# Another order for the attention of layer 0: after a run of half-width matmuls TensorE takes other full-width work ahead of new stick-breaking logits

## The chip, the cores and the metric

The kernel runs on one core of one Trainium2 chip. The metric is the device time of one execution in microseconds; the time before is the median of three runs. TensorE is written PE, VectorE DVE, ScalarE ACT, GpSimd POOL, and the engine whose queue issues most transfers SP.

## What is computed

A decoder trunk of two layers on 2,074 positions (16 learned meta tokens, 2,048 real ones, and padding). Only layer 0's attention is touched by the change. It has two groups of eight heads that read the same input, a stick-breaking attention and an MLA softmax attention:

```
def stick_breaking_attention(q, k, v):
...
        z = jnp.einsum('bthd,bshd->bhts', q[:, q0:q1], k[:, :q1]).astype(jnp.float32) * scale
...
        log_beta = jax.nn.log_sigmoid(z)
        log_1m = jnp.where(mask, log_beta - z, 0.0)
        suffix = lax.cumsum(log_1m, axis=3, reverse=True) - log_1m
        a = jnp.where(mask, jnp.exp(log_beta + suffix), 0.0)
        outs.append(jnp.einsum('bhts,bshd->bthd', a.astype(v.dtype), v[:, :q1]))
...
def causal_block_softmax_attention(q, k, v, scale):
...
        p = jax.nn.softmax(jnp.where(mask, s, NEG), axis=-1)
        outs.append(jnp.einsum('bhts,bshd->bthd', p.astype(v.dtype), v[:, :q1]))
```

The suffix sum makes a stick-breaking block depend on the block after it along the keys, so the key blocks of one query group are worked one after the other. The softmax has no such chain.

## The kernel before, in words

The program has three large parts one after the other: the projections of layer 0, its attention (here the stage from 722 to 1560 us of the profiled execution), and its output projection with all of layer 1. The change acts on the attention alone.

The 17 blocks of 122 positions are cut into query groups, one of one block (group 0) and four of four blocks (groups 1 to 4, 488 columns wide). The eight heads of each kind are worked as four pairs. For a pair and a group the kernel goes through steps, one key block of each kind a step; group 4 has 17 steps, group 3 has 13, then 9, 5 and 1. The groups of a pair run from 4 down to 0 (in the last pair 4, 0, 3, 2, 1). The first four steps of a long group are on the diagonal, so their stick-breaking part has 122, 244, 366 and 488 columns; all later ones have 488.

One step gives these operations, each for head m = 0 and 1 of the pair (the kinds are the names in the planner's tables):

- qks: stick-breaking logits, two matmuls into a PSUM tile zp (L1048, L1049); z masks the diagonal (L1056, DVE).
- e: softplus of zp into sp (L1060, ACT); c: one row of sp is overwritten with the running sum of the step before, read from that step's zp (L1067, ACT); h: sp rounded (L1075 on DVE, or L1073 on ACT); lo: the rest, sp minus h, into l (L1080, POOL or DVE).
- tri: two matmuls that add the triangular sums of h and l into the same zp (L1085, L1086); a: the weights from zp (L1090, ACT).
- qkm: MLA logits, three matmuls into ms (L1118 to L1120); p: their exponent (L1124, ACT); pm masks the diagonal (L1130, DVE); acc adds p up for the denominator (L1136, L1138, POOL).
- avs and avm: the products with the values, for both heads at once (L1098, L1146). Each head has 64 outputs, so each of these matmuls uses half of PE's columns: these, and dn (L1158, the denominators), are the half-width ones. The trace shows four records for one avs or avm, all other matmuls are full-width with one record.

So there is a chain per head: tri of a step, then c, h, lo and tri of the next step, with PE, ACT, DVE and POOL in turn.

The order is not written by hand. attention_plan makes the 4,320 operations with costs, dependences and the buffers that each takes and frees (two zp tiles for each head, for example), and list_schedule plays them through: whenever an engine is free it takes the ready operation with the smallest key. The key is the step's number plus RANK of the kind. A half-width operation gets RANK's few added when fewer than two of its sort are ready, and RANK's stay taken off while PE is in a run of them, which keeps half-width work together; TURN is what the planner charges for entering a run. MOVE says how long the owning engine must still be busy before lo or acc goes to its other engine. The order that comes out is binding on PE, ACT, DVE and POOL. SP's queue is not planned here; it follows the order in which the loads are written, which is where their operations stand in the plan: a group's q tile (a DMA from d_sq) is loaded when the last qks of the group before the last has been placed, since there are two q buffers; mq likewise behind qkm. The keys and values of the next pair are loaded when groups 4, 3 and 2 of the current pair are done (RELOAD), so there are such loads during the first three pairs and none during the last.

Of the kernel before, what the change touches and what calls it, by code (L numbers as in the profile page):

```python
# [126 lines left out]
def attention_plan():  # L127
# [115 lines left out]
    for o in ops:  # L243
        for d, w in o.deps:
# [4 lines left out]
DMA_NS = 6000  # L249
RINGS = dict(zp0=2, zp1=2, a0=3, a1=3, sp0=2, sp1=2, h0=2, h1=2, l0=2, l1=2, av=1, mav=1, ms=2,  # L250
             p0=3, p1=3, acc0=3, acc1=3, og=2, rd=1)
RANK = dict(qks=-48.53, z=-16.4, e=36.5, rc=-42.98, c=-9.66, h=11.42, lo=-30.91, tri=-5.03, a=4.01, avs=5.07, avm=3.11, ogs=23.02, qkm=-2.2, p=-10.76, pm=2.07, acc=-41.78, ogm=12.82, dn=-0.45, rd=8.86, rm=-7.51, head=0.23, other=11.93, few=12.47, stay=8.39)
MOVE = dict(lo=829, acc=3122, h=0)
HEAD = {("lo", "tri"): -200, ("a", "avs"): -40, ("p", "avm"): -40}
HALF_WIDTH = ("avs", "avm", "dn")
TURN = 342
# [5 lines left out]

def list_schedule(ops, rank=RANK, move=MOVE, rings=RINGS):

    engines = ("PE", "ACT", "DVE", "Pool")
    held = {r: [] for r in rings}
    users, wait, rt, pri = {}, {}, {}, {}
    ready = {e: [] for e in engines}
    for i, o in enumerate(ops):
        wait[o], rt[o] = len(o.deps), 0  # L270
        pri[o] = (o.s.i + rank[o.kind] + rank["head"] * o.m, i)
        for b in o.rel:
            users[b] = b.users
        if not o.deps:
            ready[o.eng].append(o)
    busy = {e: 0 for e in engines}
    out, events, tick, now, half = [], [], 0, 0, False
    while len(out) < len(ops):
        again = True
        while again:  # L280
            again = False
            for e in engines:
                if busy[e] > now:
                    continue
                best = None
                if e == "PE":
                    few = rank["few"] * (sum(o.kind in HALF_WIDTH and rt[o] <= now for o in ready[e]) < 2)
                for src in engines:
                    for o in ready[src]:
                        own = src == e  # L290
                        if rt[o] > now or not own and (not o.alt or o.alt[0] != e or busy[src] - now < move[o.kind]):
                            continue
                        if any(len(held[b.ring]) >= rings[b.ring] and users[held[b.ring][-rings[b.ring]]] for b in o.acq):
                            continue
                        k = (pri[o][0] + (0 if own else rank["other"]), pri[o][1])
                        if o.kind in HALF_WIDTH:
                            k = (k[0] - rank["stay"] if half else k[0] + few, k[1])
                        if best is None or k < best[0]:
                            best = (k, o, src)
                if best:  # L300
                    _, o, src = best
                    ready[src].remove(o)
                    for b in o.acq:
                        held[b.ring].append(b)
                    o.on, o.start = e, now
                    o.took = o.cost if src == e else o.alt[1]
                    if e == "PE":
                        o.took += TURN * (o.kind in HALF_WIDTH and not half)
                        half = o.kind in HALF_WIDTH
                    busy[e] = now + o.took  # L310
                    tick += 1
                    heapq.heappush(events, (busy[e], tick, "end", o))
                    out.append(o)
                    again = True
        if not events:
            break
        while True:
            now, _, what, x = heapq.heappop(events)
            if what == "end":
                for y, w in x.outs:  # L320
                    wait[y] -= 1
                    rt[y] = max(rt[y], now + w + LAT[x.on, y.eng])
                    if wait[y] == 0:
                        ready[y.eng].append(y)
                        tick += 1
                        heapq.heappush(events, (rt[y], tick, "ready", y))
                for b in x.rel:
                    tick += 1
                    heapq.heappush(events, (now + 200, tick, "free", b))
            elif what == "free":  # L330
                users[x] -= 1
            if not events or events[0][0] > now:
                break
    assert len(out) == len(ops)
    return out
# [5 lines left out]
def build(tc, a, off, upto=99):  # L341
# [113 lines left out]
    b2 = ExitStack()  # L455
    MSC = float((NOPE + ROPE) ** -0.5)
    plan = list_schedule(attention_plan())
    groups = sorted({o.s.G.i: o.s.G for o in plan}.values(), key=lambda g: g.i)
    slots = dict(big=0, small=0)
# [1462 lines left out]
```

## Time and profile before

| | |
|---|---|
| three runs | 2561.8, 2563.64 (median), 2575.18 us |
| profiled execution | 2566.46 us, its span 2564.7 us |
| attention in it | 722 to 1560 us |
| PE, DVE, ACT, POOL busy over the span | 98%, 59%, 51%, 41% |
| TensorE clock granted, mean | 0.995 |

Matmuls are pipelined: the next one starts while the last is still in the array, and a record's length is more than the distance to the next start. So "busy" says little about PE here, and the distances between starts say what a matmul costs. An idle time that is printed for PE is what is left after the modelled end of the matmul before; the distance of the starts is longer.

### The profile page before, as it was taken

Reading aid. Unit: us, or ns where it says so; the run is one execution under the profiler, and the core shown is the slowest. Engines: PE = TensorE matmul, PEld = TensorE weight load, DVE = VectorE, ACT = ScalarE, POOL = GpSimd, SP = SyncE. Lnnn points to the kernel's source line nnn. Section 1 sums busy time; section 2 is a strip of 40 time slices with the busy share of each in tenths; the row PEclk is TensorE's granted clock in tenths of the full one; section 3 lists DMA queues with packets and bytes.
Section 4 is the critical chain, followed back from the end, with each engine's and each line's share of the span. In section 5 each row is a group of like instructions: output and inputs, shape, how many; then the busy total and the mean of one; then the engine's idle time right before and its main releaser. Section 6 shows DMA issues by size and latency. Waiting matters only on the chain.

```text
span 2564.7 us, 38785 instructions
## 1 busy us (share of the span) xinstructions
PE 2525.8 (98%) x13105; PEld 1968.7 (77%) x13105; DVE 1523.6 (59%) x3356; ACT 1313.0 (51%) x3347; POOL 1042.5 (41%) x848
## 2 busy tenths in 40 slices
PE   9999999999999999999999999999999999999998
PEld 7887888999966666666666666788999888777776
DVE  5365486878435565565575665434222678888874
ACT  6532121213258878878878783423222577665442
POOL 1022200010058878878878776300000123356552
PEclk9999999999999999999999999999999999999999
DMA  5476744342576361252330214534554455676652
GB/s 149 108 200 174 198 115 109 93 119 81 132 166 146 82 157 44 78 144 51 91 102 22 66 61 143 168 91 139 128 124 120 123 134 137 162 206 190 202 164 92
DMA packets 337857, 321.29 MB, mean 125 GB/s; under 512 B 143670, under 2 KB 319738, under 8 KB 337075
## 3 DMA queue, kind: packets, MB, share of 16 engines
q1 hardware_dynamic: 336939, 317.56, 46.0%
q8 instruction: 103, 1.69, 0.3%
q10 hardware_dynamic: 720, 1.26, 0.1%
q14 instruction: 95, 0.78, 0.1%
HBM read 198.28 MB, written 120.80 MB: 124 GB/s over the span
## 4 chain that ended last, share of the span: by engine, by line
PE 90%; DVE 3%; DMA 3%; SPq 1%; issue 1%; ACT 1%; POOL 1%; ACTq 0%; DVEq 0%; POOLq 0%
PE psd L419 8%; PE psd L420 8%; PE psd L421 8%; PE pso L1797 7%; PE psg L1684 6%; PE av L1098 5%; PE mav L1146 5%; PE zp L1048 4%; PE psx L967 3%; PE zp L1086 3%; PE zp L1085 3%; PE zp L1049 3%; PE pso L1275 2%; PE ms L1118 2%; PE pso L1273 2%; PE ms L1119 2%
## 5 line engine op out<-in xcount | busy, mean ns | idle before, releaser
L1624 POOL TENSOR_TENSOR s_sb<-s_sb,den 108x1008 f32<-108x1008 f32 (+1 forms) x76 | 151.7, 1995 | 513.4 <-DVE den L1623 459.0
L1080 POOL TENSOR_TENSOR l<-sp,h 123x488 fp32r<-123x488 f32 (+3 forms) x253 | 292.9, 1164 | 106.1 <-DVE h L1075 86.9
L1075 DVE CAST h<-sp 123x488 fp32r<-123x488 f32 (+3 forms) x266 | 178.4, 676 | 252.7 <-ACT sp L1067 234.3
L1138 POOL TENSOR_TENSOR acc<-acc,p 122x488 f32<-122x488 f32 (+3 forms) x288 | 313.5, 1108 | 31.8 <-DVE p L1130 24.8
L419 PE MATMUL psd<-xh,wh 128*128 128x366 f32 (+1 forms) x760 | 274.3, 361 | 0.0
L421 PE MATMUL psd<-xh,wl 128*128 128x366 f32 (+1 forms) x760 | 268.0, 353 | 0.0
L420 PE MATMUL psd<-xl,wh 128*128 128x366 f32 (+1 forms) x760 | 267.7, 352 | 0.0
L1060 ACT ACTIVATE sp<-zp 123x488 f32<-123x488 f32 (+3 forms) x360 | 173.1, 515 | 60.3 <-DVE zp L1056 30.5
L1090 ACT ACTIVATE a<-zp 123x488 f32<-123x488 f32 (+3 forms) x360 | 168.2, 503 | 40.9 <-PE zp L1086 24.3
L1067 ACT ACTIVATE sp<-zp 1x488 f32<-1x488 f32 (+3 forms) x320 | 154.3, 497 | 40.6 <-PE zp L1086 36.7
L1615 ACT ACTIVATE s_sb<-s_sb,nm 108x252 f32<-108x252 f32 (+1 forms) x304 | 149.4, 495 | 31.3 <-DVE nm L1606 31.1
L1124 ACT ACTIVATE p<-ms 122x488 f32<-122x488 f32 (+3 forms) x320 | 150.6, 513 | 22.7 <-PE mav L1146 20.2
L420 PEld LDWEIGHTS psd<-xl,wh 128*128 128x128 f32 x760 | 144.1, 190 | 15.9 <-issue 0.9
L419 PEld LDWEIGHTS psd<-xh,wh 128*128 128x128 f32 x760 | 144.1, 190 | 12.5 <-issue 0.7
L421 PEld LDWEIGHTS psd<-xh,wl 128*128 128x128 f32 x760 | 143.4, 189 | 10.9
L1080 DVE TENSOR_TENSOR l<-sp,h 123x488 fp32r<-123x488 f32 (+3 forms) x107 | 133.6, 1253 | 16.8 <-ACT h L1073 13.3
L1048 PEld LDWEIGHTS zp<-q,kbig 128*123 128x123 f32 x320 | 59.0, 184 | 110.0 <-ACT a L1090 60.7
L1098 PE MATMUL av<-a,vbig 123*64 123x488 f32 (+3 forms) x640 | 142.3, 522 | 0.0
L1146 PE MATMUL mav<-p,mvbig 122*64 122x488 f32 (+3 forms) x640 | 142.2, 522 | 0.0
L409 POOL TENSOR_TENSOR wl<-raw,wh 128x1024 fp32r<-128x1024 f32 x17 | 40.9, 2404 | 244.4 <-DVE wh L408 159.2
L1604 DVE CUSTOM_DVE_ANT_0 s_sb<-pss,bt,sinks 108x252 f32<-108x252 f32 (+1 forms) x304 | 127.5, 474 | 20.7 <-PE pss L1601 11.6
L1048 PE MATMUL zp<-q,kbig 128*123 128x488 f32 (+3 forms) x320 | 127.1, 401 | 5.9 <-DMA q<-d_sq 2.6
(516 smaller groups left out, 6774.7 us busy)
## 6 DMA issues: line engine op xcount, KB each, us to landing
kbig<-d_sk SPq DMA_DIRECT2D x32, 492.0 KB
q<-d_q SPq DMA_DIRECT2D x36, 432.0 KB
xt<-in_x SPq DMA_DIRECT2D x32, 448.0 KB
raw<-in_od_w_in SPq DMA_DIRECT2D x48, 256.0 KB
mq<-d_mq SPq DMA_DIRECT2D x32, 373.6 KB
raw<-in_ev_w_in SPq DMA_DIRECT2D x19, 512.0 KB
kkb<-d_kk SPq DMA_DIRECT2D x18, 472.0 KB
xt<-d_h SPq DMA_DIRECT2D x16, 512.0 KB
```

The lines of the kernel that those rows point to most:

```text
L419: T.matmul(o, wh[:, k, m0:m1], xh[:, k, c0:c1], start=(k == 0), stop=False)
L420: T.matmul(o, wh[:, k, m0:m1], xl[:, k, c0:c1], start=False, stop=False)
L421: T.matmul(o, wl[:, k, m0:m1], xh[:, k, c0:c1], start=False, stop=(k == k_n - 1))
L1048: T.matmul(zp[:BC, :s.ns], k[:, 2 * m, c], q, start=True, stop=False)
L1060: S.activation(sp[:BC, :s.ns], s.zp[m][:BC, :s.ns], AF.Softplus)
L1075: V.tensor_copy(h[:BC, :n], sp[:BC, :n])
L1080: on_(on).tensor_tensor(l[:BC, :n], s.sp[m][:BC, :n], f(s.h[m][:BC, :n]), op=ALU.subtract)
L1090: S.activation(x[:BC, :s.ns], s.zp[m][:BC, :s.ns], AF.Softplus)
L1098: T.matmul(s.G.av[64 * m:64 * m + 64, s.js:s.G.n], v[:BC, bi, 64 * m:64 * m + 64], s.a[m][:BC, :s.ns], start=s.first, stop=s.last, skip_gr ...
L1138: eng.tensor_tensor(g.acc[m][:BK, s.jm:g.n], g.acc[m][:BK, s.jm:g.n], s.pt[m][:BK, :n], op=ALU.add)
L1146: T.matmul(s.G.mav[64 * m:64 * m + 64, s.jm:s.G.n], v[:BK, bi, 64 * m:64 * m + 64], s.pt[m][:BK, :s.nm], start=s.first, stop=s.last)
L1797: T.matmul(ps, l[:, k], r[:, k, c], start=(k == 0 and x == 0), stop=(k == KT - 1 and x == 2))
```

## The change

Two things. RANK and MOVE get other numbers, so the planner makes another order out of the same operations. And list_schedule gets one rule more: while PE is in a run of half-width matmuls (half is true), a qks has RANK's new after (82.24) added to its key, so that other ready full-width work, tri or qkm, is taken first. No operation is added or taken away, no cost, buffer or dependence changes; of the operations that may run on two engines some change sides (h: 94 of 360 on ACT before, 71 now; lo: 107 of 360 on DVE before, 96 now; all 288 acc stay on POOL).

```
-RANK = dict(qks=-48.53, z=-16.4, e=36.5, rc=-42.98, c=-9.66, h=11.42, lo=-30.91, tri=-5.03, a=4.01, avs=5.07, avm=3.11, ogs=23.02, qkm=-2.2, p=-10.76, pm=2.07, acc=-41.78, ogm=12.82, dn=-0.45, rd=8.86, rm=-7.51, head=0.23, other=11.93, few=12.47, stay=8.39)
-MOVE = dict(lo=829, acc=3122, h=0)
+RANK = dict(qks=-82.73, z=-19.33, e=53.35, rc=-55.88, c=-5.38, h=33.35, lo=-36.74, tri=-4.7, a=13.49, avs=3.36, avm=3.18, ogs=3.02, qkm=-3.86, p=-33.02, pm=31.57, acc=-36.77, ogm=8.85, dn=-23.47, rd=7.46, rm=-19.38, head=1.02, other=15.51, few=38.0, stay=6.83, after=82.24)
+MOVE = dict(lo=764, acc=5968, h=0)
...
                         k = (pri[o][0] + (0 if own else rank["other"]), pri[o][1])
+                        if half and o.kind == "qks":
+                            k = (k[0] + rank["after"], k[1])
                         if o.kind in HALF_WIDTH:
```

Behind line 294 of the new kernel all line numbers are two higher, so L1048 of before is L1050 of after.

Counted over the whole attention, PE's order has 168 runs of half-width matmuls before and 151 after, with the same 380 avs, avm and dn in them: before 67 runs hold one of these operations, 24 two, 49 three, 25 four and 3 six; after it is 9, 92, 19, 28 and 3. Behind such a run stood a qks 158 times and a tri 9 times; now a tri stands there 149 times and a qks once.

First place, PE in the middle of the second pair's group 3, where all tiles are 488 wide. Before, a run that holds one avm (mav), and the new logits behind it:

```order
L1120 MATMUL ms<-mq,mkbig_8421 122x488
L1146 MATMUL mav<-p_10161,mvbig_8423 64x488
L1146 MATMUL mav<-p_10166,mvbig_8423 64x488
L1048 MATMUL zp_10295<-q,kbig_8890 123x488
L1049 MATMUL zp_10295<-q,kbig_8890 123x488
L1048 MATMUL zp_10302<-q,kbig_8890 123x488
L1049 MATMUL zp_10302<-q,kbig_8890 123x488
L1085 MATMUL zp_10255<-h_10279,tri_r 123x488
```

Behind the run come both heads' qks (L1048, L1049), then a tri (L1085). After, at the same place:

```order
L1122 MATMUL ms<-mq,mkbig_8384 122x488
L1148 MATMUL mav<-p_10071,mvbig_8877 64x488
L1148 MATMUL mav<-p_10078,mvbig_8877 64x488
L1100 MATMUL av<-a_10118,vbig_7719 64x488
L1100 MATMUL av<-a_10159,vbig_7719 64x488
L1087 MATMUL zp_10143<-h_10184,tri_r 123x488
L1088 MATMUL zp_10143<-l_10199,tri_r 123x488
L1050 MATMUL zp_10221<-q,kbig_8383 123x488
```

The run holds an avm and an avs, and a tri (L1087, L1088) that needs h and l stands first behind it.

Second place, ACT in the first steps of the second pair's group 4 (the third and fourth step; tiles widen from 244 to 488). Before, from p of the third step's second head to h of the fourth step's first head:

```order
L1124 ACTIVATE p_9175<-ms 122x488
L1090 ACTIVATE a_9177<-zp_9072 123x244
L1060 ACTIVATE sp_9182<-zp_9140 123x366
L1124 ACTIVATE p_9191<-ms 122x488
L1067 ACTIVATE sp_9182<-zp_9072 1x244
L1124 ACTIVATE p_9198<-ms 122x488
L1060 ACTIVATE sp_9206<-zp_9179 123x488
L1067 ACTIVATE sp_9206<-zp_9131 1x366
L1090 ACTIVATE a_9225<-zp_9131 123x366
L1073 ACTIVATE h_9231<-sp_9206 123x488
```

After, from p of the third step's first head to the same h:

```order
L1126 ACTIVATE p_9156<-ms 122x488
L1126 ACTIVATE p_9161<-ms 122x488
L1062 ACTIVATE sp_9172<-zp_9133 123x366
L1092 ACTIVATE a_9174<-zp_9087 123x244
L1069 ACTIVATE sp_9172<-zp_9087 1x244
L1126 ACTIVATE p_9182<-ms 122x488
L1062 ACTIVATE sp_9190<-zp_9158 123x488
L1126 ACTIVATE p_9194<-ms 122x488
L1069 ACTIVATE sp_9190<-zp_9114 1x366
L1062 ACTIVATE sp_9205<-zp_9187 123x488
L1075 ACTIVATE h_9211<-sp_9190 123x488
```

The last row is what lo and then tri of the fourth step wait for. On PE that tri (zp_9158) now stands ahead of the fifth step's qks; before, tri (zp_9179) stood behind them.

Third place, SP's queue at the end of the first pair, up to the load of the second pair's first q tile. Before:

```order
L357 DMA kbig3_10063<-d_sk2_67 64x4x492
L357 DMA mq_8870<-d_mq_69 98x2x488 x2
L1109 DMA d_og2_84<-og_8887 128x488
L357 DMA sg_8904<-d_sg0_74 128x122
L357 DMA sg_8904<-d_sg4_78 128x122
L357 DMA mq_8930<-d_mq_69 98x2x488 x2
L357 DMA q_8964<-d_sq1_62 128x2x488
```

The two loads of mq_8930, which belong to the group after, go out right ahead of q_8964. After:

```order
L359 DMA sg_8888<-d_sg0_74 128x122
L359 DMA sg_8888<-d_sg4_78 128x122
L1174 DMA d_og2_84<-og_8807 128x488
L359 DMA kbig3_10026<-d_sk2_67 64x4x492
L359 DMA mq_8898<-d_mq_69 98x2x488 x2
L359 DMA q_8943<-d_sq1_62 128x2x488
L359 DMA kbig3_10026<-d_sk2_67 64x4x492
L359 DMA mq_8982<-d_mq_69 98x2x488 x2
```

The next group's mq_8982 now stands behind the q tile that is waited for (q_8943).

## The prediction

> **What bounds the kernel now.** First the profile page, for the whole span:
>
> ```profile
> span 2564.7 us, 38785 instructions
> PE 2525.8 (98%) x13105; PEld 1968.7 (77%) x13105; DVE 1523.6 (59%) x3356; ACT 1313.0 (51%) x3347; POOL 1042.5 (41%) x848
> PE 90%; DVE 3%; DMA 3%; SPq 1%; issue 1%; ACT 1%; POOL 1%; ACTq 0%; DVEq 0%; POOLq 0%
> ```
>
> The chain that ended last lies on PE for 90% of its length. Then the attention alone, in the view by windows (columns: window, its length, each engine's busy time, granted clock, DMA share, GB/s):
>
> ```profile
> 722.00:1560.00 838.00, 827.28 (x4063) 514.54 (x4061) 499.75 (x757) 658.27 (x1517) 661.54 (x598) 1.00 0.36 91
> ```
>
> ACT and POOL are busy for 79% of these 838 us, PE all the time. They are not the bound on average, but near enough to be it for some microseconds. As a busy PE may still lose time between matmuls, I read the starts in the timeline. A run of one half-width operation, a run of three, and neighbours of 366 and 244 columns:
>
> ```profile
> 987.97 0.39 PE L1120 MATMUL ms<-mq,mkbig 96*122 96x488 f32 x1
> 988.28 1.04 PE L1146 MATMUL mav<-p,mvbig 122*64 122x488 f32 x4
> 989.80 0.39 PE L1048 MATMUL zp<-q,kbig 128*123 128x488 f32 x1
> ...
> 992.27 0.39 PE L1120 MATMUL ms<-mq,mkbig 96*122 96x488 f32 x1
> 992.58 1.04 PE L1098 MATMUL av<-a,vbig 123*64 123x488 f32 x4
> 993.45 0.99 PE L1146 MATMUL mav<-p,mvbig 122*64 122x488 f32 x4
> 994.27 0.99 PE L1098 MATMUL av<-a,vbig 123*64 123x488 f32 x4
> 995.74 0.38 PE L1048 MATMUL zp<-q,kbig 128*123 128x488 f32 x1
> 995.96 0.39 PE L1049 MATMUL zp<-q,kbig 128*123 128x488 f32 x1
> ...
> 997.07 0.34 PE L1118 MATMUL ms<-mq,mkbig 98*122 98x366 f32 x1
> 997.24 0.33 PE L1119 MATMUL ms<-mq,mkbig 96*122 96x366 f32 x1
> ...
> 1000.57 0.28 PE L1118 MATMUL ms<-mq,mkbig 98*122 98x244 f32 x1
> 1000.69 0.28 PE L1119 MATMUL ms<-mq,mkbig 96*122 96x244 f32 x1
> ```
>
> A full-width matmul of 488 columns costs 0.22 us (995.74 to 995.96), one of 366 costs 0.17, one of 244 costs 0.12. From the last full-width start before a run to the third one behind it are 1.83 us with one half-width operation (987.97 to 989.80) and 3.47 us with three (992.27 to 995.74). Two operations more cost 1.64 us, so one costs 0.82. The rest, 1.83 - 0.82 - 3 x 0.22 = 0.35, is the price of entering and leaving a run, whatever its length. Last, PE's waits in the attention (waiter, what ended the wait, us in total, times, longest):
>
> ```profile
> PE zp L1048 <- DMA q<-d_sq: 2.6, 2, 1.7
> PE zp L1048 <- DMA kbig<-d_sk: 2.2, 1, 2.2
> PE zp L1086 <- DVE l L1080: 1.4, 7, 0.2
> PE zp L1048 <- ACT sp L1067: 1.0, 2, 0.5
> PE ms L1118 <- ACT sp L1067: 0.6, 2, 0.4
> PE ms L1118 <- ACT acc L1124: 0.6, 1, 0.6
> ```
>
> In 838 us PE waits 4.8 us for transfers and 3.6 us for other engines. So only the entries and these few waits can be won.
>
> **Fewer runs.** The order has 168 runs before and 151 after. 17 x 0.35 = 5.9 us less. It counts in full, because PE has nothing else to do in that time. That a tri stands behind the run now, and not a qks, changes nothing in this price as long as h and l are there:
>
> ```profile
> 1139.00 0.38 PE L1146 MATMUL mav<-p,mvbig 122*64 122x122 f32 x4
> 1139.31 0.48 PE L1085 MATMUL zp<-h,tri_r 123*123 123x488 f32 x1
> 1139.63 0.39 PE L1086 MATMUL zp<-l,tri_r 123*123 123x488 f32 x1
> 1139.91 0.27 PE L1086 MATMUL zp<-l,tri_r 123*123 123x122 f32 x1
> 1141.92 0.29 PE L1048 MATMUL zp<-q,kbig 128*123 128x122 f32 x1 [1.74 <-DMA q<-d_sq]
> ```
>
> Behind this mav the two matmuls of a tri start 0.32 us apart, 0.1 more than in a full-width row, which is part of the 0.35, and no wait is marked.
>
> **The q tile at the start of a pair.** The last row above is one of the two waits for q: the second pair's is the other. In the chain of waits their loads stand so (start, length):
>
> ```profile
> 927.11 7.33 DMA q<-d_sq
> 1133.67 8.11 DMA q<-d_sq
> ```
>
> The load goes out when the last qks of the group before the last is over, and the first qks of the new pair needs it. By the matmuls that the order puts between them, at the prices above, PE had 6.1 us of work there and has 7.1 now. The load also gets shorter: in SP's queue the next group's two mq loads are no longer ahead of it. The fourth pair starts with the same 6.1 us before and shows no wait; there no keys of a further pair are in the queue. I take both waits as gone, 2.6 us. If the load stays as long as it was, 7.3 and 8.1 against 7.1 leave 1.2 us.
>
> Behind the second of these waits the clock dropped (window, length, busy times, clock):
>
> ```profile
> 725.50:1142.81 417.31, 410.51 (x2017) 256.03 (x2016) 246.70 (x373) 331.62 (x761) 330.97 (x300) 1.00 0.48 116
> 1142.81:1146.22 3.41, 3.41 (x12) 2.02 (x13) 1.81 (x5) 2.12 (x8) 2.07 (x3) 0.50 0.92 211
> ```
>
> 3.41 us at half the clock are 1.7 us lost, and they go with the wait. The longer wait of 2.2 us for kbig, which lies in the first window, left the clock at 1.00, so a wait of about 2 us drops it at one time and not at another. [...] I go by the row: the drop came with the wait, and a new wait of about 2 us may bring one too, which I keep for the upper end.
>
> **The first keys.** The wait for kbig falls on the fifth step's qks. The load stands in the same place of SP's queue and lands when it did. In the new order a qkm (three matmuls, 0.66 us) has gone behind this qks and an avs of 122 columns (0.82 x 122 / 488 = 0.2 us) has come ahead of it, so PE arrives 0.4 to 0.5 us earlier and waits that much longer: 0.4 us more.
>
> **The start of a long group.** The ACT order of the second place is what could cost most. Mean times of one instruction, in the attention (ns behind the busy time):
>
> ```profile
> L1060 ACT ACTIVATE sp<-zp 123x488 f32<-123x488 f32 x256 | 137.1, 577 | 36.5 <-PE zp L1049 27.3 <-DVE zp L1056 6.8 <-POOL l L1080 1.6
> L1124 ACT ACTIVATE p<-ms 122x488 f32<-122x488 f32 x224 | 120.0, 573 | 16.0 <-PE mav L1146 14.5 <-PE ms L1120 0.9
> L1073 ACT ACTIVATE h<-sp 123x488 fp32r<-123x488 f32 x46 | 27.9, 607 | 1.1
> L1060 ACT ACTIVATE sp<-zp 123x366 f32<-123x366 f32 x32 | 14.8, 464 | 18.2 <-DVE zp L1056 18.2
> L1067 ACT ACTIVATE sp<-zp 1x366 f32<-1x366 f32 x32 | 14.7, 460 | 10.4 <-PE zp L1086 10.0
> L1090 ACT ACTIVATE a<-zp 123x244 f32<-123x244 f32 x32 | 11.2, 354 | 0.0
> L1067 ACT ACTIVATE sp<-zp 1x244 f32<-1x244 f32 x32 | 11.2, 351 | 1.4 <-POOL og L1171 1.3
> L1080 DVE TENSOR_TENSOR l<-sp,h 123x488 fp32r<-123x488 f32 x58 | 81.4, 1404 | 16.3 <-ACT h L1073 13.1
> ```
>
> The eleven ACT instructions from p of the third step to h of the fourth are four p and two sp of 488, one h, and one each of the last four ACT rows: 4 x 0.573 + 2 x 0.577 + 0.607 + 0.464 + 0.460 + 0.354 + 0.351 = 5.7 us. Then lo on DVE, 1.4 us: 7.1. PE can release the first p when qkm of the third step is done. From there to the second matmul of the fourth step's tri the new order has 20 matmuls of 488 columns, 4 of 366, 2 of 244 and a short run of four half-width tiles (0.8 us with its entry): 4.4 + 0.7 + 0.2 + 0.8 = 6.1 us. So this tri is at least 1.0 us late, and ACT comes into the stretch with a queue of its own. Before, PE had the fifth step's qks, two more qkm and an avm ahead of this tri; there the waits on l come to 1.4 us over the whole attention. Three pairs start like this. I take 1.5 us each, 4.5 us, half above the bare sum for the queue and the hops between engines; the bounds are 0 (ACT drains it) and 3 us each.
>
> **What lies beside other work.** 23 h go from ACT to DVE and 11 lo from DVE to POOL; on ACT 24 of 488 columns at 0.607 us are 14.6 us less, against a slack of 180. The other q and mq loads keep 20 us and more of PE work as lead, but one: the last pair's group 3, whose q had 8.8 us and has 6.1. The fourth pair's start shows that 6.1 suffices in that pair; if its load took 8.1 us, it would cost 2.0. All this I cost at nothing; if POOL's cover were gone, 11 lo at DVE's 1.4 us would be 15 us, but POOL idles for 176.
>
> **The sum.** -5.9 (runs) - 2.6 (q) - 1.7 (clock) + 0.4 (kbig) + 4.5 (starts) = -5.3 us. Against the profiled execution's 2566.46 us (span 2564.7) that is 2561.2. That execution is 2.8 us above the median of the three runs, 2563.64, and against the median it is **2558.3 us**.
>
> **The rivals.**
> Rival 1, no new waits: the short ACT stretch drains, and only the gains stand, -5.9 - 2.6 - 1.7 + 0.4 = -9.8, 2553.8 us. For it: ACT idles 21% of the stage. Against it: the bare sum is late already.
> Rival 2, the starts jam: 3 us at each of three starts, and the clock drops behind each, 3 x (3 + 1.7) = 14.1 in place of 4.5: +4.3, 2567.9 us. For it: the drop behind a 2 us wait. Against it: it needs waits in one piece.
> Rival 3, slower: a tri behind a run waits for its l. A qks needed only a free zp, which it nearly always had; a tri needs a chain over four engines. 149 runs end in one now, so from 10.2 / 149 = 0.07 us each the other terms (-5.9 - 2.6 - 1.7) are eaten; at 0.2 us each, the longest wait on an l in the table, it is 149 x 0.2 - 5.3 = +24.5, 2588 us. Against it: in the steady part a qkm and a run stand between the other head's tri and this one, over 5 us, and before, the waits on l come to 1.4 us in all.
> Rival 4, the order changes little: the gain of the runs alone is paid back by waits spread over the stage, 0 to -3 us, 2562 us.
>
> **How the numbers follow.** Forecast (2555 to 2562) 0.5, rival 1 0.17, rival 2 0.12, rival 3 0.06, rival 4 0.15. No change is within 0.5%, 12.8 us, which is about what a measurement of this kernel can tell. Only rival 1 with its remaining 3.6 us of waits gone too reaches below 2550.8: faster 0.08. Rival 3 is above 2576.5: slower 0.05. Same 0.87. The range goes from 2550, below rival 1, to 2568, rival 2's.
>
> **What would show it.** Right: the distance of starts over a run is still 0.35 us above the work in it; no wait for q at 927 and 1134 and a clock of 1.00 there; waits on l at three starts of 1 to 2 us. Wrong: many short waits of L1088 on l behind runs, waits on sp or zp in the steady part, a half clock behind the starts, or an attention that is longer than 838 us.

## The result, and the profile after

The changed kernel takes 2586.16 us (median of 6 runs, 2581.41 to 2588.97), the kernel before in the same comparison 2565.26 us (6 runs, 2561.8 to 2575.18). The ratio is 1.0078 with a 95% interval from 1.0067 to 1.0089: about 20 us slower, where 2558.3 and at most 2568 were forecast. The profiled execution took 2588.97 us. Its page has these lines:

```profile
span 2587.1 us, 38657 instructions
PE 2537.0 (98%) x13105; PEld 1970.7 (76%) x13105; DVE 1576.5 (61%) x3368; ACT 1295.0 (50%) x3324; POOL 1051.8 (41%) x859
PE 84%; DVE 5%; ACT 3%; DMA 3%; POOL 2%; issue 2%; SPq 1%; ACTq 0%; DVEq 0%; POOLq 0%
```

The span is 22.4 us longer. PE has lost six points of the chain that ended last, and VectorE, ScalarE and GpSimd have taken them. From the start of its first matmul to the start of the first one of the output projection the attention takes 855.2 us, before 835.3: 20.0 of the 22.4 us are there. The view by windows, over 858 us in place of 838:

```profile
722.00:1580.00 858.00, 837.11 (x4064) 515.67 (x4062) 547.23 (x768) 640.39 (x1494) 671.81 (x609) 1.00 0.36 89
```

ScalarE has 18 us less work than before, VectorE 47 us more. First the price of a run, in the timeline of PE. From the last full-width start ahead of the run (990.68) to the third one behind it (992.52) are 1.84 us; 0.82 + 3 x 0.22 are work, 0.36 the price, as before:

```profile
990.68 0.39 PE L1122 MATMUL ms<-mq,mkbig 96*122 96x488 f32 x1
991.00 1.04 PE L1100 MATMUL av<-a,vbig 123*64 123x488 f32 x4
991.97 0.49 PE L1087 MATMUL zp<-h,tri_r 123*123 123x488 f32 x1
992.30 0.38 PE L1088 MATMUL zp<-l,tri_r 123*123 123x488 f32 x1
992.52 0.39 PE L1050 MATMUL zp<-q,kbig 128*123 128x488 f32 x1
```

PE's waits in the attention (waiter, what ended the wait, us in total, times, longest):

```profile
PE zp L1050 <- ACT sp L1069: 6.0, 8, 3.1
PE zp L1088 <- POOL l L1082: 3.3, 9, 0.8
PE zp L1050 <- DMA kbig<-d_sk: 2.7, 1, 2.7
PE zp L1088 <- DVE l L1082: 2.2, 10, 0.3
...
PE ms L1120 <- ACT acc L1126: 1.7, 2, 0.9
...
PE zp L1050 <- DMA q<-d_sq: 0.2, 1, 0.2
```

The waits for q are gone but for 0.2 us. The waits on l are 5.5 us in place of 1.6, those of a qks for ScalarE's c (which must have read a zp before its buffer can be written again) 6.0 in place of 1.0. This view lists only part of the loss. If every start of PE is held against the prices that the prediction used, 26 us more lie above them than before: the 20.0 us by which the attention got longer, and the 5.9 that the fewer runs save.

One of these waits is long, in the last pair, and there the clock dropped; the drop that stood behind the q wait at 1142.81 is gone:

```profile
1449.66:1456.49 6.83, 5.39 (x15) 4.59 (x16) 3.73 (x8) 4.46 (x12) 3.21 (x4) 0.50 0.50 154
```

The others are short and come back at the same place of each group. From its first qks to that of the next group, a group of 13 steps in the first three pairs takes about 62.3 us in place of 60.3, one of 9 steps 42.2 in place of 40.2, though each has one run less. What has changed with them stands in the view by lines with the shapes kept apart (the mean in ns stands behind the busy time). Before:

```profile
L1138 POOL TENSOR_TENSOR acc<-acc,p 122x488 f32<-122x488 f32 x192 | 246.5, 1303 | 19.0 <-DVE p L1130 11.9 <-ACT p L1124 7.0
L1075 DVE CAST h<-sp 123x488 fp32r<-123x488 f32 x210 | 143.4, 690 | 218.8 <-ACT sp L1067 212.1 <-POOL acc L1138 5.4
L1075 DVE CAST h<-sp 123x366 fp32r<-123x366 f32 x24 | 23.6, 984 | 15.5 <-ACT sp L1067 15.4
L1067 ACT ACTIVATE sp<-zp 1x488 f32<-1x488 f32 x224 | 120.2, 557 | 18.1 <-PE zp L1086 16.8
L1075 DVE CAST h<-sp 123x244 fp32r<-123x244 f32 x16 | 7.7, 480 | 13.7 <-POOL acc L1136 7.0 <-ACT sp L1067 6.8
```

And after:

```profile
L1140 POOL TENSOR_TENSOR acc<-acc,p 122x488 f32<-122x488 f32 x192 | 258.2, 1362 | 7.8 <-DVE p L1132 4.6 <-ACT p L1126 3.0
L1077 DVE CAST h<-sp 123x488 fp32r<-123x488 f32 x234 | 197.8, 847 | 210.6 <-ACT sp L1069 191.9 <-PE ms L1122 15.0 <-POOL l L1082 1.4
L1069 ACT ACTIVATE sp<-zp 1x488 f32<-1x488 f32 x224 | 124.0, 560 | 71.1 <-PE zp L1088 69.9
L1077 DVE CAST h<-sp 123x244 fp32r<-123x244 f32 x28 | 24.8, 884 | 15.3 <-ACT sp L1069 15.1
```

The same copy of 488 columns takes 847 ns in place of 690, that of 244 columns 884 in place of 480. The timeline says why. This is the start of a group of nine steps, rows of VectorE, then GpSimd, ScalarE and PE:

```profile
1084.87 1.25 DVE L1077 CAST h<-sp 123x244 fp32r<-123x244 f32 x1 [0.79 <-ACT sp L1069]
1086.04 0.28 DVE L1058 TENSOR_TENSOR zp<-zp,cp 123x122 f32<-123x122 f32 x1
1087.18 1.11 DVE L1077 CAST h<-sp 123x244 fp32r<-123x244 f32 x1 [0.86 <-ACT sp L1069]
1088.22 0.28 DVE L1058 TENSOR_TENSOR zp<-zp,cp 123x122 f32<-123x122 f32 x1
...
1084.73 1.24 POOL L1138 TENSOR_TENSOR acc<-acc,p 122x488 f32<-122x488 f32 x1 [0.76 <-ACT p L1126]
1086.92 1.22 POOL L1138 TENSOR_TENSOR acc<-acc,p 122x488 f32<-122x488 f32 x1
...
1086.41 0.37 ACT L1062 ACTIVATE sp<-zp 123x244 f32<-123x244 f32 x1 [0.99 <-DVE zp L1058]
1088.53 0.48 ACT L1062 ACTIVATE sp<-zp 123x366 f32<-123x366 f32 x1 [1.45 <-DVE zp L1058]
...
1087.13 0.43 PE L1050 MATMUL zp<-q,kbig 128*123 128x366 f32 x1 [0.38 <-ACT sp L1069]
1091.04 0.43 PE L1088 MATMUL zp<-l,tri_r 123*123 123x366 f32 x1 [0.30 <-POOL l L1082]
```

A copy of 244 columns that starts just behind an acc of GpSimd ends 0.15 us behind it: 1086.12 against 1085.97, and 1088.29 against 1088.14. With GpSimd idle it takes 0.29 us. Behind the copy in VectorE's queue stands the zmask of the next logits, which then holds up sp on ScalarE, c, the free zp and the l of the step after: PE waits at 1087.13 and 1091.04. Sorted by what runs beside them, copies of 488 columns take 0.41 us when GpSimd is idle (40 of 234); 100 of the 234 took over 1 us, before 50 of 210. Each of these 100 began while a GpSimd instruction was running and ended 0.27 or 0.28 us behind that instruction's end, so its length is set by how much of that instruction was left. VectorE's instructions with one operand in PSUM (zmask, which is the z of the list above, and the two products into og, the tile in which a group's output times its gate waits for its store) take the same beside GpSimd and alone: 0.28 us for 122 columns, 0.60 to 0.67 for 488.

What in the chip holds a copy back until then, no run of this case shows.

### The profile page after: what moved, and what is told of

Its sections match the earlier page's. It is cut to its first block, busy times and chain, and to the rows that moved or that the text cites. A ratio compares the mean times of both kernels' runs of the same rounds, so it can differ in the third digit from the quotient of the medians.

```text
span 2587.1 us, 38657 instructions
## 1 busy us (share of the span) xinstructions
PE 2537.0 (98%) x13105; PEld 1970.7 (76%) x13105; DVE 1576.5 (61%) x3368; ACT 1295.0 (50%) x3324; POOL 1051.8 (41%) x859
## 3 DMA queue, kind: packets, MB, share of 16 engines
q10 hardware_dynamic: 720, 1.26, 0.1%
## 4 chain that ended last, share of the span: by engine, by line
PE 84%; DVE 5%; ACT 3%; DMA 3%; POOL 2%; issue 2%; SPq 1%; ACTq 0%; DVEq 0%; POOLq 0%
PE psd L421 8%; PE psd L422 8%; PE psd L423 8%; PE pso L1799 7%; PE psg L1686 7%; PE mav L1148 4%; PE av L1100 3%; PE psx L969 3%; PE zp L1087 3%; PE pso L1277 2%; PE pso L1275 2%; PE pso L1276 2%; PE zp L1088 2%; PE av L1650 2%; PE zp L1050 2%; PE pt L1636 2%
## 5 line engine op out<-in xcount | busy, mean ns | idle before, releaser
L1077 DVE CAST h<-sp 123x488 fp32r<-123x488 f32 (+3 forms) x289 | 238.2, 825 | 238.6 <-ACT sp L1069 215.1
L1140 POOL TENSOR_TENSOR acc<-acc,p 122x488 f32<-122x488 f32 (+3 forms) x288 | 329.1, 1160 | 20.1 <-DVE p L1132 17.0
L1092 ACT ACTIVATE a<-zp 123x488 f32<-123x488 f32 (+3 forms) x360 | 172.5, 497 | 42.2 <-PE zp L1088 39.3
L1087 PEld LDWEIGHTS zp<-h,tri_r 123*123 123x123 f32 x360 | 66.2, 184 | 104.0 <-DVE h L1077 38.7
L1087 PE MATMUL zp<-h,tri_r 123*123 123x488 f32 (+3 forms) x360 | 143.5, 399 | 0.0
L1088 PE MATMUL zp<-l,tri_r 123*123 123x488 f32 (+3 forms) x360 | 133.9, 372 | 6.9 <-POOL l L1082 3.3
L1606 DVE CUSTOM_DVE_ANT_0 s_sb<-pss,bt,sinks 108x252 f32<-108x252 f32 (+1 forms) x304 | 127.4, 474 | 20.6 <-PE pss L1603 11.5
```

The lines of the kernel that those rows point to most:

```text
L1077: V.tensor_copy(h[:BC, :n], sp[:BC, :n])
L1087: T.matmul(z[:BC, :n], rnd["tri"][:BC], s.h[m][:BC, :n], start=False, stop=False, skip_group_check=True)
L1088: T.matmul(z[:BC, :n], rnd["tri"][:BC], s.l[m][:BC, :n], start=False, stop=True, skip_group_check=True)
L1140: eng.tensor_tensor(g.acc[m][:BK, s.jm:g.n], g.acc[m][:BK, s.jm:g.n], s.pt[m][:BK, :n], op=ALU.add)
```

## The experiments

Four theories. **Chain**: tri, c, h, lo and the next tri of a head follow too closely in the new order (the core of rival 3). **One place**: the long wait in the last pair is most of it. **Collision**: VectorE's copies meet GpSimd's work. Within it, **how many** (23 more h on VectorE) or **when** (the order).

**The chain cut.** In both orders c takes row 0 from its own step's logits, as many instructions of the same size; the running sum of the step before is left out:

```diff
-            S.activation(s.sp[m][0:1, n - k:n], s.prev.zp[m][0:1, :k], AF.Copy, scale=-1.0 / CW)
+            S.activation(s.sp[m][0:1, n - k:n], s.zp[m][0:1, n - k:n], AF.Softplus)
```

The changed order:

> The changed kernel with the link between two steps of a head cut: c takes row 0 from the step's own logits in place of those behind the tri of the step before (as many instructions of the same size; the carry of the stick-breaking is left out). Theory 'chain' (PE waits because tri of one step, c, h, lo and tri of the next follow too closely in the new order): the waits on l and on zp of about 25 us go, the kernel falls by 18 to 28 us to 2558 to 2568, below or at the kernel before. Theory 'collision' (VectorE and GpSimd are slowed and late whatever c waits for): it falls by less than 8 us, 2578 or more.

The order before:

> The kernel before with the same link cut (the carry is left out). Theory 'chain': the old order has few waits of this kind, so it gains 2 to 6 us, 2559 to 2563; the cut version of the changed kernel is then 4 to 8 us faster than it, which is the gain from fewer runs and from the q tiles. Theory 'collision': the cut versions stay about 20 us apart, the changed one slower.

Measured: 2581.62 us for the changed order, ratio to before 1.0072 (1.0057 to 1.0087); 2563.35 for the old one, 0.9997 (0.9987 to 1.0007). The idle time ahead of c fell from 71.1 us to 1.6. Part of the wait went to a, which waits for the same tri on ScalarE (90.6 us in place of 41.7), so the cut is not complete:

```profile
L1069 ACT ACTIVATE sp<-zp 1x488 f32<-1x488 f32 x224 | 122.8, 555 | 1.6
L1092 ACT ACTIVATE a<-zp 123x488 f32<-123x488 f32 x256 | 146.0, 571 | 90.6 <-PE zp L1088 86.6 <-PE av L1100 2.5
```

The waits on l stayed:

```profile
PE zp L1088 <- POOL l L1082: 7.2, 16, 0.8
PE zp L1088 <- DVE l L1082: 2.3, 10, 0.3
```

The two orders remain 18 us apart. That speaks against the chain theory, and with it against the mechanism of rival 3. As the cut is not complete, the run with another h below decides: there the chain is whole.

**The long wait.** In the trace after it begins with VectorE, which waits 3.65 us for the store of an earlier og before it may write the next one into the same buffer. Rows of VectorE, ScalarE, PE:

```profile
1449.86 0.28 DVE L1110 TENSOR_TENSOR og<-av,sg 128x122 f32<-128x122 f32 x1 [3.65 <-DMA d_og<-og]
1450.07 0.28 DVE L1058 TENSOR_TENSOR zp<-zp,cp 123x122 f32<-123x122 f32 x1
...
1450.38 0.37 ACT L1062 ACTIVATE sp<-zp 123x244 f32<-123x244 f32 x1 [4.00 <-DVE zp L1058]
1450.79 0.26 ACT L1069 ACTIVATE sp<-zp 1x122 f32<-1x122 f32 x1
...
1451.10 0.67 PE L1050 MATMUL zp<-q,kbig 128*123 128x366 f32 x1 [3.11 <-ACT sp L1069]
```

The edit gives og a third buffer:

```diff
-            og = work("og", 2)
+            og = work("og", 3)
...
-            og = s.G.og = work("og", 2)
+            og = s.G.og = work("og", 3)
```

> The changed kernel with three og buffers in place of two. In the trace after, the longest wait of PE in the attention (3.27 us at 1451.1, half clock for 6.83 us around it) follows a VectorE multiply into og that waits 3.65 us for the store of an earlier og; the zmask behind it and the softplus behind that are late. Theory 'one place' (this wait is a cost of its own): 3.3 + 3.4 = about 6.7 us less than the changed kernel, 2579 to 2581 us, the rest of the loss stays. Theory 'late anyway' (the chain would hold PE up there without the store too): less than 2 us gained.

Measured: 2582.3 us, ratio 1.0073 (1.0056 to 1.0091). In its trace this wait and its drop are gone and the attention takes 850.7 us, 4.5 less, though a drop of 3.41 us stands at 738.16, at the wait for kbig (the keys), where the trace after has none. So in the traces this place is a cost of its own. The medians lie 3.9 us apart, between the two theories, and the ratio against the changed kernel's 1.0078 cannot tell the gain from nothing; most of the loss is elsewhere.

**Another h.** sp is the softplus of the logits in zp, so it is never less than they are, and row 0 of zp is zero at that point. The larger of the two is sp, and the instruction has one operand in PSUM:

```diff
-                V.tensor_copy(h[:BC, :n], sp[:BC, :n])
+                V.tensor_tensor(h[:BC, :n], sp[:BC, :n], s.zp[m][:BC, :n], op=ALU.max)
```

The changed order:

> The changed kernel with h on VectorE written as the larger of sp and the logits (in PSUM), which is sp, in place of a copy. In the traces VectorE instructions with one operand in PSUM take 0.60 to 0.67 us for 488 columns beside GpSimd and alone, while the copy takes 0.41 alone and up to 1.5 beside GpSimd (mean 0.85 after, 0.69 before). Theory 'collision': h falls to 0.65, GpSimd is no longer held up by it, and the kernel gains 10 us or more (2576 or less). Theory 'chain by position': only the 0.2 us of h are gained where the chain is late, some 85 places, 4 to 8 us with the zp waits: 2578 to 2582. If neither: within 2 us of the changed kernel.

The order before:

> The kernel before with h on VectorE as the larger of sp and the logits. There the copy takes 0.69 us in the mean, GpSimd's lo 1.30, and PE's waits on l are 1.4 us. Theory 'the new order brings the collisions': the old order gains 0 to 3 us, 2562 to 2565, and the changed kernel with this h (2561.3) is 0 to 4 us below it, which is all that the order itself is worth. Theory 'this h helps any order': it gains 10 us or more, 2555 or less, and the new order stays behind the old one.

Measured: 2561.33 us for the changed order, ratio 0.9990 (0.9980 to 0.9999); 2563.37 for the old one, 0.9988 (0.9980 to 0.9997). One instruction's form takes 0.88% off the changed kernel, about 23 us, and 0.12%, 3 us, off the old one. That is the collision theory's result. The chain theory falls here: in this trace c still waits 69.3 us, nearly all of it for the tri of the step before, and the loss is gone all the same. In the trace of the changed order with this h:

```profile
PE 93%; DMA 2%; DVE 2%; ACT 1%; SPq 1%; issue 1%; POOL 1%; ACTq 0%; POOLq 0%; DVEq 0%
```

```profile
L1140 POOL TENSOR_TENSOR acc<-acc,p 122x488 f32<-122x488 f32 x192 | 249.2, 1312 | 14.0 <-DVE p L1132 7.0 <-ACT p L1126 6.4
L1077 DVE TENSOR_TENSOR h<-sp,zp 123x488 fp32r<-123x488 f32 x234 | 153.7, 661 | 260.7 <-ACT sp L1069 245.6 <-PE ms L1122 11.6 <-ACT a L1092 2.6
L1077 DVE TENSOR_TENSOR h<-sp,zp 123x244 fp32r<-123x244 f32 x28 | 11.3, 404 | 14.8 <-ACT sp L1069 14.7
```

PE has 93% of the chain, before the change 90%. The 234 h of 488 columns on VectorE take 0.65 to 0.67 us each, whatever GpSimd does. In the first three pairs a group of 13 steps takes about 60.2 us and one of 9 steps 39.8, where it was 62.3 and 42.2. The place shown above now reads (VectorE, GpSimd, PE):

```profile
1075.54 0.41 DVE L1077 TENSOR_TENSOR h<-sp,zp 123x244 fp32r<-123x244 f32 x1 [0.77 <-ACT sp L1069]
1077.00 0.41 DVE L1077 TENSOR_TENSOR h<-sp,zp 123x244 fp32r<-123x244 f32 x1 [0.85 <-ACT sp L1069]
1077.52 1.26 DVE L1082 TENSOR_TENSOR l<-sp,h 123x244 fp32r<-123x244 f32 x1
...
1075.41 1.24 POOL L1138 TENSOR_TENSOR acc<-acc,p 122x488 f32<-122x488 f32 x1 [0.76 <-ACT p L1126]
1077.28 1.23 POOL L1138 TENSOR_TENSOR acc<-acc,p 122x488 f32<-122x488 f32 x1
...
1077.27 0.34 PE L1050 MATMUL zp<-q,kbig 128*123 128x366 f32 x1
```

The first h runs its 0.41 us right through an acc, PE starts that qks without a wait. The l of 244 columns, with both operands in SBUF, is still held up by the second acc (1.26 us; the one at 1088.41 in the trace after, with GpSimd idle, took 0.40).

**A longer h.** A second such instruction on 122 columns stands behind each:

```diff
                 V.tensor_tensor(h[:BC, :n], sp[:BC, :n], s.zp[m][:BC, :n], op=ALU.max)
+                V.tensor_tensor(h[:BC, :BK], sp[:BC, :BK], s.zp[m][:BC, :BK], op=ALU.max)
```

> The changed kernel with h as the larger of sp and the logits, and a second such instruction on 122 columns behind each: h then takes about 0.66 + 0.2 = 0.86 us of VectorE for 488 columns, the mean of the copy after the change (0.85), but never more, and neither holds GpSimd up nor is held up by it. Theory 'length' (PE waits because h is longer by 0.15 to 0.2 us in the mean): most of the loss is back, 2578 or more. Theory 'collision' (it is the copies of 1.0 to 1.5 us, and the zmask, l and GpSimd work that stand behind them): 2562 to 2569.

Measured: 2568.68 us, ratio 1.0007 (0.9998 to 1.0016). In its trace the two instructions take 0.98 us from the start of the first to the end of the second, not the 0.86 expected, and so more than the copy's mean of 0.85. The 0.3 us on each h cost 0.17%, about 4 us; the mean length of the copy is the small part of the loss, its long cases and what stands behind them the large part.

**How many, or when.** Each order was run with the engines that the other one gives to h, and then to lo, by two sets of step numbers:

```diff
+                if o.kind == "h":
+                    o.on = "ACT" if 2 * o.s.i + o.m in H_ACT else "DVE"
                 RUN[o.kind](o.s, o.m, *([o.on] if o.alt else []))
```

The changed order with the old engines for h:

> The order of the changed kernel, with each h on the engine that it had before (94 on ScalarE in place of 71, of them 46 of 488 columns in place of 22). Theory 'more h on VectorE': most of the 21 us come back, 2565 to 2573. Theory 'the order' (the copies meet GpSimd's work because of when they come, not how many they are): less than 6 us, 2580 or more.

The old order with the new engines for h:

> The order of the kernel before, with each h on the engine that it has after the change (289 on VectorE in place of 266). Theory 'more h on VectorE': 10 to 20 us slower than before, 2575 to 2585. Theory 'the order': within 4 us of before, 2561 to 2569.

The changed order with the old engines for h and lo:

> The order of the changed kernel with each h and each lo on the engine that it had before. With h's engines alone it stood at 2577.3, 12 us above before. Theory 'order' (the copies and GpSimd's work meet because of when the new order sends them): it stays there, 2572 to 2582. Theory 'lo': the 11 more lo on GpSimd are what is left, it falls to 2562 to 2568. Theory 'matched sides' (sides taken from another order fit badly, so that part of the 12 us is due to the mixing): it gets slower than 2580.

The old order with the new engines for lo:

> The order of the kernel before with each lo on the engine that it has after the change (96 on VectorE in place of 107). Theory 'lo': 6 to 12 us slower than before. Theory 'lo costs nothing', as predicted: within 3 us of before. Theory 'matched sides': 5 to 15 us slower, since 71 lo on VectorE stand at other places than the order made them for.

Measured, in that order: 2577.29 (1.0053, 1.0037 to 1.0068), 2576.78 (1.0050, 1.0036 to 1.0064), 2580.06 (1.0061, 1.0045 to 1.0076) and 2583.24 (1.0064, 1.0048 to 1.0081). The first lies between its two theories, 12 us above before and 9 below the changed kernel. The second, 11 us above before, falls where more h on VectorE was to bring it. The third stands at the border of its first theory and that of matched sides. The last one warns against reading them: it is 17 us slower although VectorE has 11 lo less; matched sides had forecast 5 to 15. An order mixed with another's engines seems to cost by itself. So three of the mixes were run again with the other h.

The old order with the new engines for h:

> The order of before with the changed kernel's engines for h, and h on VectorE as the larger of sp and the logits. With the copy this mix stood 11 us above before. Theory 'copies': those 11 us are copies that meet GpSimd's work, and go: 2561 to 2567, beside the 2563.4 of the old order with this h. Theory 'mix' (work sent to an engine whose queue was ordered without it comes late whatever its length): most of them stay, 2571 or more.

The old order with the new engines for lo:

> The order of before with the changed kernel's engines for lo, and h as the larger of sp and the logits. With the copy this mix stood 17 us above before. Theory 'copies': 2561 to 2567. Theory 'mix': 2574 or more.

The changed order with the old engines for h:

> The changed order with the engines that h had before, and h on VectorE as the larger of sp and the logits. With the copy this mix stood 12 us above before, 9 below the changed kernel. Theory 'copies': 2559 to 2564, as the changed kernel with this h (2561.3). Theory 'mix': 2570 or more.

Measured: 2574.13 (1.0028, 1.0019 to 1.0038), 2575.37 (1.0027, 1.0016 to 1.0039) and 2567.07 (0.9997, 0.9986 to 1.0008). The two mixes of the old order stay 0.4% above that order with this h (0.9988): mixing does cost there, about 10 us, as the theory of that name said. The mix of the new order lies between its two theories. What can be read is the price of the copy, the ratio with it less the ratio without it, in each arrangement:

| order | engines of h | h of 488 columns on VectorE | of them over 1 us | with copy | without | price, us |
|---|---|---|---|---|---|---|
| before | before | 210 | 50 | 1 | 0.9988 | 3 |
| before | after | 234 | 53 | 1.0050 | 1.0028 | 6 |
| after | before | 210 | 68 | 1.0053 | 0.9997 | 14 |
| after | after | 234 | 100 | 1.0078 | 0.9990 | 23 |

The intervals of two ratios together leave about 4 us on each price, and some 6 on the difference of two prices. The order (with its own engines for lo) raises the price by 11 and by 17 us; the 24 copies more raise it by 3 in the old order, which the runs cannot tell from nothing, and by 8 in the new one, which is hardly more than the 6. So it is chiefly when the new order sends the copies, and the count of long copies in the four traces goes the same way. No single move of the order was singled out, and the new rule for qks and the new numbers of RANK were not run apart.

**Both edits.** The changed order with this h and three og buffers:

> The changed kernel with both edits that helped: h as the larger of sp and the logits, and three og buffers. With h alone, PE still waits 1.6 us at the start of the last pair's second group and half a clock of 3.41 us stands there. The third buffer brought 3.9 us to the changed kernel alone; here 1.6 + 1.7 = 3.3 at most: 2558 to 2561, 4 to 7 us below the kernel before. If the third buffer's gain was the collision's: no less than 2561.

Measured: 2560.0 us, ratio 0.9976 (0.9968 to 0.9985), the fastest of all, 6 us below before. Whether the third buffer adds to the 0.9990 of h alone is at the edge of the two intervals.

## Why the prediction was wrong, point by point

- **Fewer runs, -5.9 us: right.** 151 runs at 0.34 to 0.36 us.
- **The q tile, -2.6: half right.** The waits fell from 2.6 to 0.2. But the load did not get shorter as I argued, and in front of it stand two qkm that wait for ScalarE, 1.7 us in place of 0.6. The gain is 1.3. The load of the third pair's q in the chain:

```profile
1139.69 8.67 DMA q<-d_sq
```

- **The clock, -1.7: the drop went, another came.** At 1449.66 there are 6.83 us at half clock, behind a wait on an og buffer. PE stood still until 1451.10, so 2.7 us of them are lost. I had followed the loads past their queues, but not the stores: og has two buffers, and the new order brings a product into one of them while its store is still under way.
- **First keys, +0.4: right.** 2.2 became 2.7.
- **Starts of long groups, +4.5: the size about right, the cause mostly another.** The groups of 17 steps of pairs 2, 3 and 4 lose 5.3 us more than before, without the q and the clock. I had it from a queue on ScalarE. With the other h, in the same order and with the same queue, about 1.3 of them are left, so the larger part is the collision's. The 1.4 us that I charged for lo on VectorE was itself such a price: with GpSimd idle it takes 0.67 us (2 of 60 in the trace after).
- **"All this I cost at nothing": the step that failed.** The prediction set 23 h that go to VectorE against ScalarE's slack and GpSimd's idle time, and never priced them where they go, nor any of the copies that stay there and that the new order sends at other times. A copy that meets GpSimd's work takes up to 1.5 us in place of 0.41, and the zmask behind it is late too. Seven long groups at whose start nothing was forecast, those of 13 and of 9 steps in the first three pairs and that of 9 in the last, lose 2.3 us more each, 16.2 us, and with the other h 0.2 at most. The group of 13 steps in the last pair adds 6.3, of them 3.3 for the og wait and 2.7 for its clock. The last group adds 2.8, of which 2.6 stay with the other h: that is not the collision, and its cause stays open. The short groups give 1.9 back.

With these the terms, in the order runs, q, the old drop, the first group (with the keys), starts, the seven groups, the group with the og wait, the last and the short ones, are -5.9 - 1.3 - 1.7 + 0.3 + 5.3 + 16.2 + 6.3 + 2.8 - 1.9 = 20.1 against the 20.0 measured. They are read from the starts of PE at the prediction's prices, group by group, in one execution of each kernel.

- **Rival 3 gave 2588 us and slower, and got 2586 by another way.** 18 of the 149 tri behind a run find l late, 6.0 us, 0.04 us each, under the rival's break-even of 0.07. More is lost at tri elsewhere (65 of 211, 10.3 us) and at qks, the cut chain changed little, and with the other h 1 of the 149 is late. Its 0.2 us each was the longest wait of the table, not a measured mean: the number agrees by chance.
- **With the other h the two orders stand level.** They are at 0.9990 and 0.9988, and the intervals leave some 3 us either way. In their profiled executions the attention takes 832.8 us in the new order, with 10.2 us of it at half clock, and 835.9 in the old one, with 13.7; without what the clock cost, 832.8 - 5.1 = 827.7 and 835.9 - 6.8 = 829.1. That is an estimate from one execution each. So even without the collisions of h nothing shows the whole of my -5.3, or of the -3.6 without the clock's 1.7 (lo on VectorE still meets GpSimd's work there, 1.16 us in the mean for 488 columns): the gain of the runs is there, and what the last group (2.6 us) and the starts (1.3) lose takes much of it back.

The sign was there to be seen. In the profile before, the copy of 366 columns takes 984 ns and that of 488 columns 690. A group whose smaller shape takes longer is not limited by its size alone, and its price may move when the order moves.

## What to carry to other kernels

Price an instruction by what runs beside it in the new order, not by its mean in the old one; a mean that does not grow with the size, as the copy's 984 ns for 366 columns against 690 for 488, says that something else holds it up. Moving work to an engine with idle time is not free when another engine can hold that work up: here VectorE's copies of 488 columns took 0.41 us with GpSimd idle and up to 1.5 beside it, where they waited for the end of its instructions, and the form with one operand in PSUM took 0.65 to 0.67 whatever GpSimd did. When an order is changed, follow the buffers of stores as well as the queues of loads.

## What the runs showed of the hardware

In the traces before and after the drops to half clock lie on a grid. Before they begin at 402.1, 1142.81 and 1562.65 us: 217 and 123 times 3.413 us apart. After, at 401.77, 1449.66 and 1582.78: 307 and 39 times. In the attention they last 3.41 or 6.83 us, and the same wait brings one or not: a wait for kbig of 2.2 us left the clock at 1.00 in one trace and halved it in another (the run with three og buffers), one of 2.7 us left it, one of 1.8 us (the cut chain in the old order) halved it. What goes with the drops is how much of the wait falls between two neighbouring points of the grid: of the 2.2 and 2.7 us that left the clock alone, 1.5 us do, of the two that halved it 2.2 and 1.8. Between 700 and 1600 us of all sixteen traces, each of the 31 stretches of the grid at full clock in which PE was idle for more than 1.61 us was followed by a drop (before and after these are 1.74 and 2.69, 1.67 and 2.28 us); of the 29 with 1.0 to 1.61 us 7 were (none of the four before and after, 1.05 to 1.50 us), of those with less none. One profile of the fastest version has 20.6 us at half clock in the whole span (mean granted clock 0.996), one of the version with the other h alone 40 (0.993): some 10 us between executions of nearly the same work, more than several of the effects told here.
